# Where the split weights lie in the on-chip memory: stationary ones 16 bytes off a multiple of 256 from the activations

## The chip, the cores and the metric

The kernel runs on one core of a Trainium2 chip. A core has a matrix engine (TensorE, PE in the profile, with its weight loads as PEld), a vector engine (DVE), a scalar engine (ACT), GpSimd (POOL), a queue engine that issues transfers (SP), and an on-chip memory of 128 partitions in which every tile is given a byte address that is the same in all partitions. The metric is the device time of one execution in microseconds (us). What a measurement of this kernel can tell from no change is about 0.2%, 3 us.

## What is computed

One layer of a transformer-like backbone on 256 latent tokens and 256 context tokens of width 2048, all in 32-bit floats:

```
mod   = silu(c) @ w_mod + b_mod              # six vectors; mod_c likewise from c_ctx
h     = rmsnorm(x) * (1 + ca) + sa ;  h_c likewise from ctx
p     = h @ w_in       # q, k, v, pooling input, gate logits; of h_c only k and v
mix   = (sigmoid(g_a) * (diff_attention(q, k, v) @ w_a_up)
       + sigmoid(g_b) * (multiscale_pool(p_pool) @ w_b_up)) @ w_o
x     = x + ga * mix
x     = x + gm * (relu(h2 @ w_ff1)^2 @ w_ff2),   h2 = rmsnorm(x) * (1 + cm) + sm
```

w_ff1 is 2048 x 8192 and w_ff2 8192 x 2048. Together the weights are some 340 MB, read once.

## The kernel before

**Split products.** The matrix engine works here on a reduced form of 32-bit numbers (F32R). To keep the accuracy, every weight chunk and every activation is split into a high half (ACT copies it into F32R, line 213 for weights) and a low half (DVE subtracts the high half from the source, line 214). A product is three matmuls: high by high, high by low, low by high, summed in a PSUM bank.

**Stream of weights.** A list, `stream`, holds all chunks of weights in the order of use, 128 partitions x 1024 numbers (4 KB in each partition) but for the small `pool_w`. `wchunk` hands out the next one and calls `load_next` so that two further chunks are loaded: a transfer into one of five `raw` tiles, the split into a tile `whi` and a tile `wlo`, each with three buffers used in turn (lines 211 and 212). Before a chunk's halves are written, the matmuls on the chunk three places earlier must be done. The chunks of the first key group go to a tile `first` instead.

**Two forms of matmul.** In a matmul one operand of 128 x 128 is loaded into the array first (stationary; the profile's LDWEIGHTS) and the other is streamed past it (moving). While one matmul streams, the load for the next goes on.

- *Weights moving.* `xstat` (lines 391 to 414), `mod_chunk` and `xmm` load activations as stationary operand and stream 512 columns of a weight half. This is so for w_m, w_q, w_k, w_v, the gates, w_a, w_b, w_o and w_ff2.
- *Weights stationary.* The pooling input (`pooling`, w_p, through `mm3`, lines 241 to 243), the first block of the MLP's first product (`ff1_first`, w_ff1a, also `mm3`) and its blocks 1 to 7 (`ff1`, w_ff1, lines 939 and 942) load 128 x 128 of a weight half and stream activations. In `ff1` one chunk gives eight matmuls of its high half with 512 columns (both halves of the activations, 256 tokens each, line 939) and then eight of its low half with 256 columns (line 942). A matmul of `mm3` streams 256 columns. `pool_w` is stationary too (`pool_out`), against the tiles `dh` and `dl`.

The order of the blocks of the MLP is first product of block b+1, then second product of block b (`ff2`, through `xstat`). In the middle of the kernel attention is interleaved with the projections.

**Addresses.** A pool gives each tag of tiles (all its buffers) one piece of the partition, in the order in which the tags first occur, each buffer rounded up to 32 bytes. In order: the parameters, two tiles of 8 KB (`s8`), seven of 16 KB (`s16`: all split activations, hL, hC, h2, mix, oT, yb and act, lie in them), then `ones` (512 bytes), `ebias` and `epsb` (4 bytes each), `mean` (512), nine `work` tiles of 2048 (`dh`, `dl`, `ah`, `al` among them), `sil` (128), twelve small tiles of 64 bytes, `tabs` (2048), `wkt` (256), `nlam` and `sub8` (4 each), two `aT` tiles of 4096, five `raw` tiles of 4096, three `whi` and three `wlo` of 4096, and `macc`. From the end of the seven large tiles to the first `whi` these are 51,456 bytes, 201 x 256. So all halves of weights lie at a multiple of 256 bytes from all split activations. The work tiles lie 512 + 32 + 32 + 512 = 1088 bytes behind the large ones, 64 more than a multiple of 256.

Of the kernel before, what the change touches and what calls it, by code (L numbers as in the profile page):

```python
# [11 lines left out]
F32 = mybir.dt.float32  # L12
F32R = mybir.dt.float32r
# [4 lines left out]
P = 128  # L18
D = 2048
KT = D // P  # L20
# [28 lines left out]
def layer(ctx: ExitStack, tc, a, out):  # L49
    nc = tc.nc  # L50
    pool = ctx.enter_context(tc.tile_pool(name="sb", bufs=1))
# [23 lines left out]
    def s16(name, shape, dt=F32):  # L75
        return pool.tile(shape, dt, tag="s16", name=name, bufs=7)

    def s8(name, shape, dt=F32):
        return pool.tile(shape, dt, tag="s8", name=name, bufs=2)

    def small(name, n):
        return pool.tile([P, n], F32, tag="sm", name=name, bufs=12)

    def pairtile(name):
        return s16(name, [P, 2, 8, T], F32R)
# [25 lines left out]
    def raw_chunk(src, n=1024):  # L111
        raw = pool.tile([P, n], F32, tag="raw", name="raw", bufs=5)
        nc.sync.dma_start(raw, src)
        return raw
# [66 lines left out]
    def x1_tile():  # L181
        if not x1s:
            x1s.append(s16("x1", [P, 2, D]))
        return x1s[0]

    loaded = []
    done = [0]

    def load_next():
        key, rate = stream[len(loaded)]  # L190
        src = a[key[0]]
        for i in key[1:]:
            src = src[i]
        if key[0] == "prq":
            nc.sync.dma_start(prq, src)
            loaded.append((key, None, None))
            return
        if key[0] in ("cT", "x"):
            dst = cT[:, 4 * key[1]:4 * key[1] + 4, :] if key[0] == "cT" else x1_tile()[:, key[1], key[2] * 512:key[2] * 512 + 512]
            nc.sync.dma_start(dst, src)  # L200
            loaded.append((key, None, None))
            return
        n = src.shape[-1]
        raw = raw_chunk(src, n)
        if key[:2] == ("w_k", 0):
            if not first:
                first.append(s16("first", [P, 4, 1024], F32R))
            i = 2 * (key[2] % 2)
            hi, lo = first[0][:, i, :], first[0][:, i + 1, :]
        else:  # L210
            hi = pool.tile([P, n], F32R, tag="whi", name="whi", bufs=3)
            lo = pool.tile([P, n], F32R, tag="wlo", name="wlo", bufs=3)
        act.copy(hi, raw)  # L213
        vec.tensor_sub(lo, raw, hi.bitcast(F32))  # L214
        loaded.append((key, hi, lo))
        credit[0] += rate
        credit_rate[0] = rate
        while credit[0] >= 1.0:
            credit[0] -= 1.0
            if late[0] is not None:  # L220
                next(late[0], None)

    def wchunk(*key, ahead=AHEAD):
        while len(loaded) < min(done[0] + 1 + ahead, len(stream)) or loaded[done[0]][1] is None:
            if loaded and done[0] < len(loaded) and loaded[done[0]][1] is None:
                done[0] += 1
                continue
            load_next()
        got, hi, lo = loaded[done[0]]
        assert got == key, (got, key)  # L230
        loaded[done[0]] = None
        done[0] += 1
        tick()
        return hi, lo
# [10 lines left out]
    def rsq(v, n, div, tag=None):  # L245

        mk = (lambda nm: small(nm, n)) if n <= 16 else (lambda nm: work(nm, [P, n]))
        y = pool.tile([P, n], F32, tag=tag, name=tag, bufs=2) if tag else mk("rq_y")
        pin(act.activation(y, v, AF.Ln, scale=div * 2.0 ** -64, bias=epsb))
        act.activation(y, y, AF.Exp, scale=-0.5, bias=ebias)  # L250
        t = mk("rq_t")
        vec.scalar_tensor_tensor(t, y, -0.5 * div, y, ALU.mult, ALU.mult)
        vec.scalar_tensor_tensor(t, v, EPS / div, t, ALU.add, ALU.mult)
        vec.scalar_tensor_tensor(y, t, 1.5, y, ALU.add, ALU.mult)
        return y
# [4 lines left out]
    nc.sync.dma_start(prm, a["prm"])  # L260
    xT = s16("xT", [P, KT, T])
    cT = s16("cT", [P, KT, T])
    for i in range(4):
        nc.sync.dma_start(xT[:, 4 * i:4 * i + 4, :], a["xT"][i])

    def pr(name):
        lo, hi = PRM[name]
        return prm[:, lo:hi]
# [5 lines left out]
    ident = pr("ident")  # L274
    ones = pool.tile([P, P], F32R, tag="ones", name="ones")
    vec.memset(ones.bitcast(F32), 1.0)
    ebias = pool.tile([P, 1], F32, tag="ebias", name="ebias")
    vec.memset(ebias, -32.0 * math.log(2.0))
    epsb = pool.tile([P, 1], F32, tag="epsb", name="epsb")
    vec.memset(epsb, EPS * 2.0 ** -64)  # L280
    mean = pool.tile([P, P], F32, tag="mean", name="mean")
    vec.memset(mean, 1.0 / P)
# [2 lines left out]
    sg = work("sg", [P, 32])  # L285
    act.activation(sg, prm[:, PRM["c"][0]:PRM["cc"][1]], AF.Sigmoid)
    tc.keep_in_program_order(act.preload_act_table_set("natural_log_exp_and_others"))
    sil = pool.tile([P, 2, KT], F32, tag="sil", name="sil")
    vec.tensor_mul(sil.rearrange("p a k -> p (a k)"), sg, prm[:, PRM["c"][0]:PRM["cc"][1]])
    cv = s8("cv", [P, KT, P], F32R)  # L290
    vec.memset(cv.bitcast(F32), 0.0)
# [1 line left out]
    act.copy(cv[:, :, 0:2], silk)  # L293
    vec.tensor_sub(cv[:, :, 2:4], silk, cv[:, :, 0:2].bitcast(F32))
    b1 = small("b1", 16)
    vec.tensor_scalar(b1, pr("bca"), 1.0, None, ALU.add)

    tabs = pool.tile([P, 4, 2, 64], F32, tag="tabs", name="tabs")
    wkt = pool.tile([P, 64], F32, tag="wkt", name="wkt")
    nlam = pool.tile([P, 1], F32, tag="nlam", name="nlam")  # L300

    sub8 = pool.tile([P, 1], F32, tag="sub8", name="sub8")
    vec.tensor_scalar(sub8, pr("subln"), 1.0 - LAM0, None, ALU.mult)

    def tables():

        vec.tensor_copy(wkt, pq("wk"))

        vec.tensor_scalar(pq("wq"), pq("wq"), 0.125, None, ALU.mult)
        for i, w in enumerate(("wq", "wk")):  # L310
            wv = pq(w)
            for t in range(2):
                vec.tensor_mul(tabs[:, 2 * i, t, :], pq("cos")[:, t * 64:t * 64 + 64], wv)
                so = tabs[:, 2 * i + 1, t, :].rearrange("p (a b f) -> p a b f", a=2, b=2)
                si = pq("sin")[:, t * 64:t * 64 + 64].rearrange("p (a b f) -> p a b f", a=2, b=2)
                wr = wv.rearrange("p (a b f) -> p a b f", a=2, b=2)
                for b in range(2):
                    vec.tensor_mul(so[:, :, b, :], si[:, :, b, :], wr[:, :, 1 - b, :])
        lm = work("lm", [P, 2, 64])
        lam2 = small("lam2", 2)  # L320
        for i in range(2):
            vec.tensor_mul(lm[:, i, :], pq(f"lq{i + 1}"), pq(f"lk{i + 1}"))
        vec.reduce_sum(lam2, lm, axis=AX.X)
        act.activation(lam2, lam2, AF.Exp)
        vec.tensor_sub(nlam, lam2[:, 1:2], lam2[:, 0:1])
        vec.tensor_scalar(nlam, nlam, -LAM0, None, ALU.add)
# [765 lines left out]
```

## Time and profile before

| | |
|---|---|
| three runs | 1519.75, 1520.18, 1520.29 us, median 1520.18 |
| profiled execution | 1519.78 us |
| its span, first to last instruction | 1517.7 us, mean granted clock 0.994 |
| PE busy | 1480.7 us of matmuls, 98% of the span |
| DVE, ACT, POOL busy | 1063.2, 755.7, 129.3 us |
| moved by DMA | 347.82 MB, mean 229 GB/s |

Matmuls are pipelined and the profile models their ends, so the durations of matmul records overlap. What tells the pace of the matrix engine is the distance from one start to the next, read from the timeline (columns: start, duration, engine, line, operation, tiles, shapes, count of merged instructions). A row of a group gives count, busy time, mean duration in ns and idle time before. A row of the windows gives the stretch, its length, the busy time of each engine with its count, the granted clock, the share of the DMA engines and GB/s.

### The profile page before, as it was taken

What the parts mean: (1) busy time and instruction counts of PE and PEld (TensorE: products, weight loads), DVE (VectorE), ACT (ScalarE), POOL (GpSimd) and SP (SyncE); (2) the same over time, 40 slices, a digit from 0 to 9 for tenths busy, and PEclk for the clock granted to TensorE, in tenths of its full rate; (3) what the DMA queues carried; (4) which work ended last, traced back from release to release, by engine and by line L of the source; (5) the groups of instructions that cost most, each with busy time, mean ns of one, the idle gap of its engine ahead of it and who ended that gap; (6) DMA issues with size and microseconds to landing.
All of it is one profiled execution on the core that took longest, in us unless ns stands there. A gap on an engine that the chain in (4) does not pass through costs nothing.

```text
span 1517.7 us, 19767 instructions
## 1 busy us (share of the span) xinstructions
PE 1480.7 (98%) x7336; PEld 1232.8 (81%) x7336; DVE 1063.2 (70%) x1280; ACT 755.7 (50%) x1007; POOL 129.3 (9%) x124
## 2 busy tenths in 40 slices
PE   7899999999989999999999999999999999999998
PEld 5677877768878888888879988888888888888887
DVE  7799878777887767666757665666666555555675
ACT  6677534556655444444444554544444454444432
POOL 0100111000140000000000100100000000000170
PEclk9899999999999999999999999999999999999999
DMA  8888668556568787788755677767777666666664
GB/s 314 310 283 308 214 215 285 177 167 193 167 216 300 254 275 272 242 295 296 235 181 168 220 251 245 232 217 244 231 241 240 202 188 193 193 187 193 184 200 142
DMA packets 97439, 347.82 MB, mean 229 GB/s; under 512 B 11072, under 2 KB 11712, under 8 KB 97344
## 3 DMA queue, kind: packets, MB, share of 16 engines
q1 hardware_dynamic: 96768, 345.49, 70.4%
q8 instruction: 57, 0.93, 0.3%
q0 software_dynamic: 576, 1.08, 0.2%
q14 instruction: 38, 0.31, 0.1%
HBM read 344.44 MB, written 2.10 MB: 228 GB/s over the span
## 4 chain that ended last, share of the span: by engine, by line
PE 88%; issue 3%; DVE 3%; DMA 3%; ACT 1%; POOL 1%; DVEq 0%; SPq 0%; ACTq 0%; POOLq 0%
PE f L939 14%; PE f L411 8%; PE f L410 8%; PE f L413 8%; PE f L942 7%; PE pg L413 4%; PE pg L410 4%; PE pg L411 4%; PE pyy L410 2%; PE wo L410 2%; PE wo L413 2%; PE wo L411 2%; PE pyy L413 2%; PE pyy L411 2%; PE v L411 2%
## 5 line engine op out<-in xcount | busy, mean ns | idle before, releaser
L214 DVE TENSOR_TENSOR wlo<-raw,whi 128x1024 fp32r<-128x1024 f32 x507 | 628.6, 1244 | 365.2 <-ACT whi L213 350.9
L213 ACT CAST whi<-raw 128x1024 fp32r<-128x1024 f32 x507 | 529.8, 1047 | 587.3 <-PE f L411 178.1
L939 PE MATMUL f<-h,whi 128*128 128x512 f32 x896 | 224.2, 392 | 0.0
L411 PE MATMUL f<-whi,act 128*128 128x512 f32 x512 | 199.3, 389 | 0.0
L410 PE MATMUL f<-whi,act 128*128 128x512 f32 x512 | 199.3, 389 | 0.0
L939 PEld LDWEIGHTS f<-h,whi 128*128 128x128 f32 x896 | 161.5, 189 | 29.1
L588 DVE SCALAR_TENSOR_TENSOR macc<-raw,sil,macc 128x1024 f32<-128x1024 f32 x128 | 166.2, 1299 | 1.4 <-DMA raw<-in_w_cm_dram 0.8
L413 PE MATMUL f<-wlo,act 128*128 128x512 f32 x512 | 136.8, 389 | 0.0
L942 PEld LDWEIGHTS f<-h,wlo 128*128 128x128 f32 x896 | 122.2, 190 | 8.7
L942 PE MATMUL f<-h,wlo 128*128 128x256 f32 x896 | 124.9, 282 | 0.0
L413 PEld LDWEIGHTS f<-wlo,act 128*128 128x128 f32 x512 | 96.1, 188 | 20.0
L411 PEld LDWEIGHTS f<-whi,act 128*128 128x128 f32 x512 | 96.1, 188 | 19.8
L410 PEld LDWEIGHTS f<-whi,act 128*128 128x128 f32 x512 | 96.1, 188 | 19.8
L410 PE MATMUL pg<-whi,hL 128*128 128x512 f32 x256 | 100.5, 393 | 0.0
L411 PE MATMUL pg<-whi,hL 128*128 128x512 f32 x256 | 99.7, 389 | 0.0
L950 POOL TENSOR_TENSOR rsq<-relu 128x512 f32<-128x512 f32 x28 | 29.2, 1042 | 537.6 <-ACT relu L949 516.7
L413 PE MATMUL pg<-wlo,hL 128*128 128x512 f32 x256 | 68.6, 390 | 2.5 <-DVE wlo L214 2.5
L413 PEld LDWEIGHTS pg<-wlo,hL 128*128 128x128 f32 x256 | 48.0, 188 | 12.9 <-DVE wlo L214 2.9
L410 PEld LDWEIGHTS pg<-whi,hL 128*128 128x128 f32 x256 | 48.1, 188 | 10.1 <-issue 0.2
L411 PEld LDWEIGHTS pg<-whi,hL 128*128 128x128 f32 x256 | 48.1, 188 | 10.1 <-issue 0.2
L410 PE MATMUL wo<-whi,mix 128*128 128x512 f32 x128 | 49.9, 390 | 0.0
L411 PE MATMUL wo<-whi,mix 128*128 128x512 f32 x128 | 49.8, 389 | 0.0
(267 smaller groups left out, 2205.1 us busy)
## 6 DMA issues: line engine op xcount, KB each, us to landing
raw<-in_w_ff_dram SPq DMA_DIRECT2D x240, 512.0 KB, 4.3
raw<-in_w_m_dram SPq DMA_DIRECT2D x64, 512.0 KB, 4.9
raw<-in_w_ga_dram SPq DMA_DIRECT2D x32, 512.0 KB, 4.6
raw<-in_w_cm_dram SPq DMA_DIRECT2D x32, 512.0 KB, 4.6
raw<-in_w_gb_in_dram SPq DMA_DIRECT2D x32, 512.0 KB, 4.5
raw<-in_w_ga_in_dram SPq DMA_DIRECT2D x32, 512.0 KB, 4.4
raw<-in_w_sm_dram SPq DMA_DIRECT2D x32, 512.0 KB, 4.7
raw<-in_w_o_dram SPq DMA_DIRECT2D x32, 512.0 KB, 4.6
```

Source lines behind the costliest of these rows:

```text
L213: act.copy(hi, raw)
L214: vec.tensor_sub(lo, raw, hi.bitcast(F32))
L410: pe.matmul(banks[t], tok(h, k, 0, tt), wt, start=k == 0, stop=False)
L411: pe.matmul(banks[t], tok(h, k, 1, tt), wt, start=False, stop=False)
L413: pe.matmul(banks[t], tok(h, k, 0, tt), wt, start=False, stop=k == 2 * nk - 1)
L588: pin(vec.scalar_tensor_tensor(acc, raw, sil[:, 0, k:k + 1], acc, ALU.mult, ALU.add))
L939: pe.matmul(ps, hi[:, kk * P:kk * P + P], both(h2, k), start=k == 0, stop=False)
L942: pe.matmul(ps[:, T:2 * T], lo[:, kk * P:kk * P + P], act_slice(h2, k, 0), start=False, stop=k == KT - 1)
L950: gp.tensor_mul(sq, r, r)
```

## The change

The order of the instructions in the source and the operations are the same; the places of tiles change.

- `whi` and `wlo` become six tags of one buffer each, 1028 numbers (4112 bytes) wide. The chunks still take them in turn, three of each. A chunk's halves start at number 0 of their tile, or at number 4 (16 bytes) if the weights are w_p, w_ff1a or w_ff1.
- The six tags are allocated right behind the seven large tiles. Between them lie small ones: four tags of three small tiles (before one tag of twelve; `small` now takes the four in turn), `ebias`, `epsb`, `nlam`, `sub8`, and `sil` widened to 224 bytes. A half tile takes 4128 bytes rounded up, three small tiles 192 and a column 32: 4352 = 17 x 256. With `sil` it is 4128 + 224 = 4352 too.
- Allocations named `place` only fix that order; nothing is written to them.

So w_p, w_ff1a and w_ff1 lie 16 bytes beyond a multiple of 256 from the activations, and all other weights in these tiles at a multiple of 256, as before. What comes behind the six tags moves: the work tiles, `aT`, `raw` and `macc` are then 32 bytes off a multiple of 256 from the large tiles.

```diff
@@ -78,8 +78,11 @@
+    smalls = [0]
+
     def small(name, n):
-        return pool.tile([P, n], F32, tag="sm", name=name, bufs=12)
+        smalls[0] += 1
+        return pool.tile([P, n], F32, tag=f"sm{smalls[0] % 4}", name=name, bufs=3)
@@ -186,6 +189,16 @@
+    STATIONARY, OFFSET = ("w_p", "w_ff1a", "w_ff1"), 4
+    chunks = [0]
+
+    def halves(n, at):
+
+        i = chunks[0] % 3
+        chunks[0] += 1
+        return [pool.tile([P, 1028], F32R, tag=f"{part}{i}", name=part, bufs=1)[:, at:at + n] for part in ("whi", "wlo")]
+
@@ -208,8 +221,7 @@
-            hi = pool.tile([P, n], F32R, tag="whi", name="whi", bufs=3)
-            lo = pool.tile([P, n], F32R, tag="wlo", name="wlo", bufs=3)
+            hi, lo = halves(n, OFFSET if key[0] in STATIONARY else 0)
@@ -260,6 +272,15 @@
+    columns = []
+    for i, name in enumerate(("ebias", "epsb", "nlam", "sub8", "sil")):
+        pool.tile([P, 1028], F32R, tag=f"{('whi', 'wlo')[i // 3]}{i % 3}", name="place", bufs=1)
+        if i < 4:
+            pool.tile([P, 16], F32, tag=f"sm{i}", name="place", bufs=3)
+        columns.append(pool.tile([P, 1 if i < 4 else 56], F32, tag=name, name=name))
+    ebias, epsb, nlam, sub8, sil = columns
+    sil = sil[:, 0:32].rearrange("p (a k) -> p a k", a=2)
@@ -274,9 +295,7 @@
-    ebias = pool.tile([P, 1], F32, tag="ebias", name="ebias")
-    epsb = pool.tile([P, 1], F32, tag="epsb", name="epsb")
@@ -285,7 +304,6 @@
-    sil = pool.tile([P, 2, KT], F32, tag="sil", name="sil")
@@ -297,9 +315,7 @@
-    nlam = pool.tile([P, 1], F32, tag="nlam", name="nlam")
-
-    sub8 = pool.tile([P, 1], F32, tag="sub8", name="sub8")
```

## The prediction

> **What bounds the kernel now.** I read the engine rows of the page first, then the costliest groups of matmuls.
>
> ```profile
> span 1517.7 us, 19767 instructions
> ...
> PE 1480.7 (98%) x7336; PEld 1232.8 (81%) x7336; DVE 1063.2 (70%) x1280; ACT 755.7 (50%) x1007; POOL 129.3 (9%) x124
> ...
> GB/s 314 310 283 308 214 215 285 177 167 193 167 216 300 254 275 272 242 295 296 235 181 168 220 251 245 232 217 244 231 241 240 202 188 193 193 187 193 184 200 142
> ...
> L939 PE MATMUL f<-h,whi 128*128 128x512 f32 x896 | 224.2, 392 | 0.0
> L411 PE MATMUL f<-whi,act 128*128 128x512 f32 x512 | 199.3, 389 | 0.0
> ...
> L942 PE MATMUL f<-h,wlo 128*128 128x256 f32 x896 | 124.9, 282 | 0.0
> ```
>
> ```profile
> L241 PE MATMUL pin<-hL,whi 128*128 128x256 f32 x128 | 37.5, 293 | 0.0
> L241 PE MATMUL f<-h,whi 128*128 128x256 f32 x128 | 37.3, 296 | 0.7 <-ACT h L65 0.7
> ```
>
> PE is busy for 98% and its matmuls in the stages of the change have no idle time ahead of them. So what counts is the distance between starts. The stages whose weights are stationary, as stretches (length, then PE, PEld, DVE, ACT and POOL busy, clock, DMA share, GB/s):
>
> ```profile
> 363.00:430.00 67.00, 63.15 (x455) 56.02 (x454) 58.61 (x81) 40.01 (x70) 18.09 (x30) 1.00 0.62 195
> ```
>
> ```profile
> 801.00:803.20 2.20, 2.20 (x12) 2.20 (x12) 2.20 (x3) 0.07 (x1) 0.00 (x0) 0.51 0.30 32
> 804.50:849.50 45.00, 45.00 (x380) 45.00 (x379) 28.30 (x31) 19.70 (x24) 0.52 (x1) 1.00 0.68 209
> 850.15:894.84 44.69, 44.69 (x258) 39.32 (x257) 31.95 (x34) 25.74 (x36) 7.21 (x7) 1.00 0.71 230
> ```
>
> In turn: the pooling input, the start and the body of the first MLP block, and one of the blocks 1 to 7 (16 chunks in 44.69 us, 2.793 us a chunk). In the last two PE is busy throughout, while DVE idles for 13 to 17 us, ACT for 19 to 25, and the DMA engines for about 30%. Now the timeline of two chunks of block 1, and the first chunk of block 2, which follows a stretch of the other form:
>
> ```profile
> 850.15 2.00 PE L939 MATMUL f<-h,whi 128*128 128x512 f32 x8
> 851.99 1.11 PE L942 MATMUL f<-h,wlo 128*128 128x256 f32 x8
> 852.95 2.00 PE L939 MATMUL f<-h,whi 128*128 128x512 f32 x8
> 854.79 1.12 PE L942 MATMUL f<-h,wlo 128*128 128x256 f32 x8
> 855.74 2.00 PE L939 MATMUL f<-h,whi 128*128 128x512 f32 x8
> ```
>
> ```profile
> 938.39 1.98 PE L939 MATMUL f<-h,whi 128*128 128x512 f32 x8
> 940.21 1.12 PE L942 MATMUL f<-h,wlo 128*128 128x256 f32 x8
> 941.16 2.00 PE L939 MATMUL f<-h,whi 128*128 128x512 f32 x8
> ```
>
> Eight matmuls of 512 columns take 1.84 us (230 ns each) behind matmuls of 256 columns, but 1.82 us (227 ns) behind a stretch of 512. Same instructions, same tiles, same full clock, idle nowhere: the pace depends on how the streams of the loads and of the moving operand stand to each other. Eight of 256 columns take 0.95 us, 119 ns each. With weights moving the pace is 1.81/8 = 0.2265 us for 512 columns:
>
> ```profile
> 985.81 0.39 PE L410 MATMUL f<-whi,act 128*128 128x512 f32 x1
> ...
> 987.62 1.07 PE L413 MATMUL f<-wlo,act 128*128 128x512 f32 x4
> ```
>
> The trace has the same form with other places of its tiles. In `pool_out` the moving `dh`, `dl` stand 64 bytes past a multiple of 256 from the stationary halves, by the order of allocation; the pooling input beside it stands at a plain multiple:
>
> ```profile
> 421.24 0.28 PE L241 MATMUL pd<-dh,whi 128*128 128x256 f32 x1
> ...
> 421.92 0.28 PE L241 MATMUL pin<-hL,whi 128*128 128x256 f32 x1
> ...
> 423.42 0.28 PE L243 MATMUL pin<-hL,wlo 128*128 128x256 f32 x1
> ...
> 424.98 0.60 PE L665 MATMUL aTp<-prm,e 128*128 128x128 f32 x4
> ```
>
> Six matmuls at 64 bytes in 421.92 - 421.24 = 0.68 us are 113 ns each; thirteen at 0 in 424.98 - 423.42 = 1.56 us are 120 ns each. The same 64 bytes with 512 columns (`ah`, `al` against `ones` and, for the load behind, hL) go the other way, 0.24 us each against 0.226:
>
> ```profile
> 244.37 0.40 PE L599 MATMUL late<-ah,ones 128*128 128x512 f32 x1
> 244.61 0.40 PE L600 MATMUL late<-al,ones 128*128 128x512 f32 x1
> 244.85 0.39 PE L410 MATMUL k<-whi,hL 128*128 128x512 f32 x1
> ```
>
> So the distance of the tiles may matter by 6% either way. At half clock nothing is lost: the first MLP block starts at a granted 0.51, and seven matmuls take 1.49 us, 213 ns each, which at full clock would be half, 107 ns.
>
> ```profile
> 801.32 0.41 PE L242 MATMUL f<-h,whi 128*128 128x256 f32 x1
> ...
> 802.81 0.41 PE L241 MATMUL f<-h,whi 128*128 128x256 f32 x1
> ```
>
> **The change part by part.** *Nothing removed or added.* The same 507 splits, transfers and 7336 matmuls run in the same order on each queue; no wait is added, and each half tile is still free again after three chunks, each small one after twelve. These edits cost 0. If a wait did come of it, the chunk behind would be late, and the cover is the idle time of ACT ahead of its splits, which ends when PE frees a half:
>
> ```profile
> ACT whi L213 <- PE f L939: 84.2, 66, 1.7
> ```
>
> 84.2 us over 66 waits are 1.3 us a wait, so up to about that much is hidden.
>
> *Moved tiles behind the halves.* `raw` now stands 32 bytes off the halves, so a split reads and writes at other distances. The trace has DVE subtractions at a distance of 0 (`wlo<-raw,whi`, 1024 columns) and of 64 (`al<-macc,ah`, 512 columns):
>
> ```profile
> L214 DVE TENSOR_TENSOR wlo<-raw,whi 128x1024 fp32r<-128x1024 f32 x503 | 625.5, 1248 | 365.2 <-ACT whi L213 350.9 <-ACT v L616 3.7 <-PE k L413 2.5
> ...
> L238 DVE TENSOR_TENSOR al<-macc,ah 128x512 fp32r<-128x512 f32 x16 | 10.6, 685 | 0.0
> ```
>
> 1.22 ns a column at 0 against 1.34 at 64 with its start-up shared by half the columns: no sign that DVE minds the distance. I take 0. If all of that were the distance, a split would cost 10% of 1248 ns, 0.12 us a chunk more or, for the other sign, less; in the MLP the 13 us that DVE idles in 16 chunks hide it, and without that cover 0.12 x 507 = 61 us would be at stake.
>
> *Weights moving.* Their distance stays 0: 0.
>
> *Weights stationary, 16 bytes off.* No row shows 16 bytes. For 256 columns the bounds are 107 ns (half-clock row at full clock) and 129 (120 as now, and 9 ns, by which the 512-column pair at 64 bytes is slower). For 512 columns they are 213 (twice 107) and 236 (that pair: 0.24 by its rounded starts; 0.235 by the modelled durations, 397 against 389 ns):
>
> ```profile
> L599 PE MATMUL late<-ah,ones x16: 397/397/501, 244.4 to 1188.1; 128*128 128x512 f32 x16
> ```
>
> (The columns are the shortest, median and longest of 16, in ns.) I take 113 and 227: these are the paces that occur in this trace wherever the streams stand well, at 64 bytes for the one and behind 512-column stretches for the other, and they are one rate, 113.3 ns for 256 columns. At 120 the load looks like the limit: 119 to 120 comes only where one load must be done per 256 columns, so a load that is held up less should bring 113.
>
> Sum at the likeliest, against the profiled 1519.78 us:
> - Blocks 1 to 7: 896/8 = 112 chunks. A chunk would take 8 x 0.2267 + 8 x 0.1133 = 2.720 us in place of 2.793, 0.073 less: 112 x 0.073 = 8.2 us.
> - First block: 3 x 8 x 16 = 384 matmuls, some 24 of them at low clock; 360 x 0.0067 = 2.4 us.
> - Pooling input: again 384, 2.6 us if all of it shows. The chain of waits there:
>
> ```profile
> by line: PE pin L243 12.0%; PE pin L242 11.8%; PE pin L241 11.8%; issue 8.5%; PE ob L674 7.7%; PE sc L646 6.3%; DMA raw<-in_w_p_dram 5.3%; DVE wlo L214 4.8%; DVE macc L588 4.3%; PE aTp L665 4.2%; POOL zb L744 1.9%; DVE mx L647 1.8%; POOL za
> ```
>
> 35.6% of 67 us, 24 us, of the 384 x 0.12 = 46 us lie on it, about half: 1.3 us. The rest is covered by DVE (58.61 of 67 us busy) and the weights of w_p.
> - Together 11.9 us: 1519.78 - 11.9 = 1507.9. The profiled run lies 0.4 us under the median of the three, so I say 1508. What is late next in the MLP is nothing: at 2.720 us a chunk the transfers need 230 x 2.793/2.720 = 236 GB/s, and the slices of the page's GB/s row reach 314.
>
> **The rivals.**
> 1. *The distance does not matter.* The loss of 7 ns per 256 columns (120 against 113) belongs to the rhythm of load and stream, not to addresses, and pool_out's 113 ns came from its start. For it: pool_out never has more than a dozen matmuls in a row, and the steady 120 may need more. Against it: the equal instructions above at 227 and 230, and the pair at 236. The same time follows if the allocation doesn't land where the sums of sizes say. Nothing then changes in the sum: 1519.8 us. The Trainium skill, page "TensorE: Matmul & The Clock Gate", section "Step-by-step: what each phase is for", says that PE has two independent read ports into the on-chip memory and that loading the next weights takes no read bandwidth from the running matmul; by that rule it would be this rival, and the trace's 227 and 230 ns of the same instruction do not agree with it.
> 2. *The offset meets the moving stream* (other side). The load's reads then fall where the moving stream reads, as in the moved pair. Place: line 939. At 236 ns and with line 942 left at 120, a chunk takes 1.888 + 0.960 = 2.848 us, 0.055 more, 112 x 0.055 = 6.2 us: 1526. If the 256-column ones rise by 9 ns too, 0.127 us in a chunk, 14.2 us, and 0.009 x (360 + 192) = 5.0 us in the others: 1539. It decides from where line 939 loses more than line 942 gains. For it the 0.24 us; against it, that these are two lone matmuls each time, with no rhythm found yet.
> 3. *All loss goes.* At 107 and 213 ns a chunk takes 2.560 us: 112 x 0.233 = 26.1, first block 360 x 0.0133 = 4.8, pooling half of 5.1: 33 us, 1486. For it only the half-clock row; against it, that neither 0 nor 64 bytes shows less than 113.
>
> **How the numbers follow.** Chances: forecast (1502 to 1514) 0.50; no change (within 3 us) 0.17; slower 0.22; all loss gone or most of it 0.11. Faster by over 0.2% (3 us, about what a measurement of this kernel can tell from no change): 0.50 + 0.11 = 0.61; within: 0.17; slower: 0.22. The range leaves out the 0.11 at 1486 and the tail of rival 2 beyond 1527 (0.05): 1500 to 1527. The likeliest case alone: 1502 to 1514. Predicted: 1508.
>
> **What would show it.** Right: the eight of line 942 span 0.91 us in the timeline in place of 0.95, those of line 939 1.81 in place of 1.84; a block's 16 chunks span 43.5 us in place of 44.69; the pooling input 113 ns apart; lines 410 to 413 at 0.2265 as before. Wrong: line 942 at 0.95 and 939 at 1.84 (rival 1), line 939 at 1.88 or more (rival 2), 1.71 and 0.86 (rival 3), or a block faster with ACT or DVE as the new wait ahead of line 939. DVE's split far from 1248 ns would break the second part.

## The result, and the profile after

| | before | after |
|---|---|---|
| median of the runs | 1519.97 us (4 runs, 1518.35 to 1520.29) | 1528.76 us (4 runs, 1524.93 to 1529.34) |
| profiled execution | 1519.78 us | 1524.93 us |
| mean of span x mean granted clock | 1508.0 us (23 executions, those beside the first experiments) | 1508.6 us (4 executions) |

After over before is 1.0056, with a 95% interval of 1.0043 to 1.0068: slower by 8.8 us, outside the predicted range and of the other sign. The profiled execution of after is the fastest of its four, so its trace accounts for 5.1 of the 8.8 us. The last row of the table is explained below: at one and the same clock the two kernels would take nearly the same time.

The page of after, its engine rows and the costliest groups that answer to those shown of before (the lines of the source have moved: the splits are 225 and 226, `mm3` 253 to 255, `ff1` 955 and 958):

```profile
PE 1483.3 (97%) x7336; PEld 1233.9 (81%) x7336; DVE 1062.7 (70%) x1280; ACT 754.9 (50%) x1007; POOL 128.2 (8%) x124
...
L226 DVE TENSOR_TENSOR wlo<-raw,whi 128x1024 fp32r<-128x1024 f32 x507 | 628.9, 1244 | 369.4 <-ACT whi L225 354.3
...
L955 PE MATMUL f<-h,whi 128*128 128x512 f32 x896 | 222.1, 390 | 0.0
...
L958 PE MATMUL f<-h,wlo 128*128 128x256 f32 x896 | 124.2, 281 | 0.0
```

The same number of matmuls and splits, and the groups of the change a little shorter: line 955 2.1 us, line 958 0.7. But PE fell from 98% to 97% of a longer span (1522.8 us). Something outside these groups became slower.

**The MLP gained, a third of what was predicted.** The timeline of after, chunks of block 1 and of block 2:

```profile
857.99 2.03 PE L955 MATMUL f<-h,whi 128*128 128x512 f32 x8
859.86 1.11 PE L958 MATMUL f<-h,wlo 128*128 128x256 f32 x8
860.81 2.02 PE L955 MATMUL f<-h,whi 128*128 128x512 f32 x8
...
946.50 1.98 PE L955 MATMUL f<-h,whi 128*128 128x512 f32 x8
948.31 1.11 PE L958 MATMUL f<-h,wlo 128*128 128x256 f32 x8
949.26 1.98 PE L955 MATMUL f<-h,whi 128*128 128x512 f32 x8
```

In blocks 2 to 7 the eight of line 955 now take 1.81 us from start to start, as predicted, and a chunk 2.76. But the eight of line 958 still take 0.95 us, not 0.91. And block 1, with the same addresses and the same instructions, found another rhythm: 1.87 + 0.95 = 2.82, slower than before's 2.793. Over the blocks 1 to 7, by the starts of line 942 (958 after) in the views of tile f:

```profile
L942 PE MATMUL f<-h,wlo x896: 277/283/283, 852.0 to 1425.9; 128*128 128x256 f32 x180
```

```profile
L958 PE MATMUL f<-h,wlo x896: 277/281/283, 859.9 to 1431.0; 128*128 128x256 f32 x180
```

573.9 us became 571.1: a gain of 2.8 us. And these rows show that block 1 began 7.9 us late.

**The loss is in the first stage.** There the matmuls of w_k, w_q and w_m (the modulation, `mod`) are interleaved. The rows of tile w_q, before and then after, with the first and the last start:

```profile
L243 PE MATMUL w_q<-whi,hL x32: 387/389/397, 36.5 to 168.0; 128*128 128x512 f32 x32
```

```profile
L255 PE MATMUL w_q<-whi,hL x32: 388/389/397, 35.9 to 176.3; 128*128 128x512 f32 x32
```

The last product of w_q is 8.3 us later. The windows of before and of after over this stage, 66 to 170 us (columns as in the prediction; the two short stretches of after are used below):

```profile
66.00:170.00 104.00, 101.45 (x446) 79.10 (x445) 94.25 (x166) 73.72 (x102) 0.00 (x0) 1.00 0.83 288
```

```profile
66.00:170.00 104.00, 95.38 (x399) 70.63 (x398) 88.29 (x150) 68.42 (x93) 0.00 (x0) 0.98 0.82 276
...
133.50:138.20 4.70, 2.35 (x8) 0.98 (x7) 3.61 (x6) 2.12 (x3) 0.00 (x0) 1.00 0.94 363
138.20:142.20 4.00, 3.97 (x10) 3.15 (x11) 3.58 (x6) 3.25 (x6) 0.00 (x0) 0.57 0.57 216
```

PE does 399 matmuls in the same 104 us in which it did 446, and is idle for 8.6 us instead of 2.6. What it waits for stands in the waits of this stretch, before and then after (who waits, for whom; us in total, times, longest):

```profile
ACT whi L213 <- PE w_q L243: 2.1, 2, 1.1
ACT whi L213 <- PE mod L347: 1.8, 4, 0.7
...
PEld mod L347 <- ACT whi L213: 1.1, 2, 0.6
```

```profile
PEld mod L363 <- ACT whi L225: 7.8, 10, 1.6
...
ACT whi L225 <- PE mod L363: 7.1, 6, 2.7
...
ACT whi L225 <- PE w_q L255: 4.9, 3, 3.9
```

ACT, which splits the chunks, now waits 12.0 us for matmuls to give back a half tile (3.9 us before), and the loads of PE wait 7.8 us for ACT (1.1 before). The chunk behind does come late, at a place where PE has nothing else ready.

**Behind some of the waits the clock falls.** The timeline of PE in after around the short stretches above (idle time before an instruction and its releaser in brackets):

```profile
135.56 0.73 PE L363 MATMUL mod<-whi,cv 128*128 128x512 f32 x2 [1.18 <-ACT whi L225]
136.82 0.73 PE L363 MATMUL mod<-wlo,cv 128*128 128x512 f32 x2 [0.53 <-DVE wlo L226]
138.23 0.92 PE L363 MATMUL mod<-whi,cv 128*128 128x512 f32 x2 [0.67 <-ACT whi L225]
138.94 0.63 PE L253 MATMUL w_k<-first,hL 128*128 128x512 f32 x1
139.37 0.63 PE L254 MATMUL w_k<-first,hL 128*128 128x512 f32 x1
```

Three waits of 0.5 to 1.2 us leave PE busy for 2.35 of 4.70 us; then the granted clock is 0.57 for 4 us, and matmuls start 0.43 us apart in place of 0.23. The profiled execution of before has the clock at 1.00 in all of 66 to 170 us. The Trainium skill, page "TensorE: Matmul & The Clock Gate", section "Why this matters for your kernels", asks to avoid idle gaps of PE of more than about 3 us between bursts; here no single gap is above 1.2 us and the clock fell.

Not every wait has this effect. In the pooling stage PE waits for ACT about as long in before as in after (timeline, before and then after), but the clock falls behind the wait in after alone (windows, in the same order):

```profile
404.62 0.66 PE L665 MATMUL aTp<-prm,e 128*128 128x128 f32 x4 [2.44 <-ACT e L651]
```

```profile
410.42 0.66 PE L681 MATMUL aTp<-prm,e 128*128 128x128 f32 x4 [2.55 <-ACT e L667]
```

```profile
405.80:409.20 3.40, 3.40 (x28) 3.26 (x28) 2.62 (x5) 1.99 (x4) 3.17 (x9) 1.00 0.33 113
```

```profile
411.70:415.10 3.40, 3.40 (x18) 3.40 (x17) 1.91 (x5) 1.19 (x3) 3.29 (x7) 0.50 0.38 130
```

This execution of after has three such stretches of half clock that before's lacks, at 138.6, 411.7 and 452.6 us, of some 3.4 us each. By estimate (half of 3.4 us) each costs 1.7 us; only the first of them lies in the first stage.

The clock is also what differs most between executions of one kernel. The span times the mean granted clock of the same execution is about what the span would be if all of it ran at full clock, since PE is busy for 97 to 98% of it. For six executions of a_off0 (below), which took from 1524.15 us (clock 0.994) to 1533.84 us (clock 0.987), this product is 1512.0 us with a standard deviation of 0.5: what differs between them is the clock. Of before the mean clock is 0.9936, of after 0.9888. So of the 8.0 us by which the mean span of after is longer (1525.8 against 1517.8), 0.6 us are in the product; the 0.0048 of clock times 1526 us is 7.3.

### The profile page after: what moved, and what is told of

Read it like the earlier page. It is cut to its first block, busy times and chain, and to the rows that moved or that the text cites. A ratio compares the mean times of both kernels' runs of the same rounds, so it can differ in the third digit from the quotient of the medians.

```text
span 1522.8 us, 19769 instructions
## 1 busy us (share of the span) xinstructions
PE 1483.3 (97%) x7336; PEld 1233.9 (81%) x7336; DVE 1062.7 (70%) x1280; ACT 754.9 (50%) x1007; POOL 128.2 (8%) x124
## 4 chain that ended last, share of the span: by engine, by line
PE 88%; DVE 4%; DMA 3%; ACT 2%; issue 2%; POOL 1%; DVEq 0%; SPq 0%; ACTq 0%; POOLq 0%
PE f L955 13%; PE f L427 8%; PE f L426 8%; PE f L429 8%; PE f L958 7%; PE pg L429 4%; PE pg L426 4%; PE pg L427 4%; DVE wlo L226 2%; PE v L426 2%; PE v L427 2%; PE v L429 2%; PE wo L429 2%; PE pyy L427 2%; PE pyy L429 2%; PE wo L426 2%
## 5 line engine op out<-in xcount | busy, mean ns | idle before, releaser
L226 DVE TENSOR_TENSOR wlo<-raw,whi 128x1024 fp32r<-128x1024 f32 x507 | 628.9, 1244 | 369.4 <-ACT whi L225 354.3
L427 PEld LDWEIGHTS pg<-whi,hL 128*128 128x128 f32 x256 | 48.2, 188 | 10.3 <-issue 0.5
L363 PE MATMUL mod<-whi,cv 128*128 128x512 f32 (+1 forms) x144 | 43.3, 391 | 7.7 <-ACT whi L225 7.5
L426 PE MATMUL wo<-whi,mix 128*128 128x512 f32 x128 | 49.9, 390 | 0.0
```

The costliest lines, as they stand in the source:

```text
L363: pe.matmul(ps[:, 0:n], cv[:, k, :], part[:, kk * n:kk * n + n], start=(k == 0 and part is hi), stop=(k == 15 and part is lo))
L426: pe.matmul(banks[t], tok(h, k, 0, tt), wt, start=k == 0, stop=False)
L427: pe.matmul(banks[t], tok(h, k, 1, tt), wt, start=False, stop=False)
```

## The experiments

The edits are shown by their main lines.

The question was first which of the two parts costs the time: the places of the tiles, or that the buffers have names. The kernel before has three buffers under one tag, and a chunk gets whichever of them is free; the kernel after has three tags of one buffer and takes them in a fixed turn. In the program of before the numbers of the `whi` buffers run 0210210210210210102102102020120120..., not always in turn. (That three buffers are used in turn, as the section on the kernel before has it, is so only after the change.) Where a chunk of w_q is held long, since its products are spread over several chunks of w_m, the other two buffers alternate past it.

**r_halves: the kernel before, with only the halves in named buffers taken in turn.** Addresses modulo 256 stay as they were.

```diff
-            hi = pool.tile([P, n], F32R, tag="whi", name="whi", bufs=3)
-            lo = pool.tile([P, n], F32R, tag="wlo", name="wlo", bufs=3)
+            i = chunks[0] % 3; chunks[0] += 1
+            hi, lo = [pool.tile([P, 1024], F32R, tag=f"{part}{i}", name=part, bufs=1)[:, 0:n] for part in ("whi", "wlo")]
```

> The kernel before, all tiles at their old addresses modulo 256, with one edit: high and low halves in three named buffers each, taken in turn, in place of any free one of three. Theory: the whole early loss of the changed kernel, 6 to 12 us over the first 170 us, time 1526 to 1532; MLP blocks as before at 44.67. Rival (buffers in turn cost nothing, the loss comes from addresses or from the small tiles): 1519 to 1522.

Measured: 1531.59 us (5 runs, 1525.69 to 1533.73), ratio 1.0078 (1.0065 to 1.0091). The windows of r_halves and its row of w_q:

```profile
66.00:170.00 104.00, 96.22 (x404) 71.48 (x403) 89.36 (x153) 69.33 (x95) 0.00 (x0) 0.98 0.83 278
...
74.00:78.00 4.00, 4.00 (x13) 3.17 (x13) 4.00 (x14) 2.55 (x5) 0.00 (x0) 0.57 0.82 282
```

```profile
L243 PE MATMUL w_q<-whi,hL x32: 387/389/402, 35.4 to 175.1; 128*128 128x512 f32 x32
```

The whole loss is there with no address moved modulo 256: 404 matmuls, PE idle for 7.8 us, the clock at 0.57 from 74 to 78 us, the last product of w_q at 175.1. Of the 10.6 us by which the mean span is longer, 3.9 are in the product of span and clock (1511.9 against 1508.0); the rest is clock (0.9892).

**r_small: the kernel before, with only the twelve small tiles as four groups of three.**

```diff
-        return pool.tile([P, n], F32, tag="sm", name=name, bufs=12)
+        count[0] += 1; return pool.tile([P, 16], F32, tag=f"sm{count[0] % 4}", name=name, bufs=3)[:, 0:n]
```

> The kernel before with one edit: the twelve small tiles as four groups of three taken in turn, in place of one group of twelve; no other tile moves. Theory: little or nothing, 1518 to 1522. Rival (the small tiles make the loss): 1526 to 1530.

Measured: 1520.04 us (11 runs), ratio 1.0001 (0.9992 to 1.001). Its window:

```profile
66.00:170.00 104.00, 100.62 (x443) 78.52 (x442) 93.43 (x164) 71.94 (x100) 1.33 (x1) 1.00 0.81 279
```

Nearly the work of before (443 matmuls), and the clock stays at 1.00. The small tiles cost nothing that can be measured. (This kernel, too, has stretches of half clock in the pooling and behind it: a mean clock of 0.91 in 394 to 414 and in 435 to 455 us.)

**a_off0: the kernel after, with the 16 bytes set to 0.** The instructions keep the order of after.

```diff
-    STATIONARY, OFFSET = ("w_p", "w_ff1a", "w_ff1"), 4
+    STATIONARY, OFFSET = ("w_p", "w_ff1a", "w_ff1"), 0
```

> The changed kernel with the one number OFFSET set from 4 to 0: same order of all instructions as the changed kernel, but the halves of the stationary weights at a plain multiple of 256 bytes from the activations. Theory (two separate effects: the 16 bytes quicken the matmuls of the MLP by about 3 us, and tying each chunk to one of three named buffers in turn makes the first 170 us some 8 to 12 us slower): the early loss stays, the pace of blocks 2 to 7 goes back from 44.16 to 44.67 us a block, time 1531 to 1533, ratio to the kernel before 1.007 to 1.009. Rival (the 16 bytes themselves cost the time, say by splits that start off a line): time back to 1519 to 1521.

Measured: 1532.83 us (6 runs, 1524.15 to 1533.84), ratio 1.0068 (1.0048 to 1.0089). Its timeline in block 3:

```profile
1045.75 2.00 PE L955 MATMUL f<-h,whi 128*128 128x512 f32 x8
1047.59 1.11 PE L958 MATMUL f<-h,wlo 128*128 128x256 f32 x8
1048.54 2.00 PE L955 MATMUL f<-h,whi 128*128 128x512 f32 x8
```

The chunk is back at 1.84 + 0.95 = 2.79 us, so the 16 bytes alone make the difference of pace. The intervals of the two ratios overlap, because of the clock; span times clock separates them: 1512.0 us against 1508.6 for after. The offset is worth 3.4 us. All that after lost, it lost without the offset.

**m_all: the tiles where after has them, 16 bytes included, but each chunk takes the buffer that it had before.** The numbers come from a written list (`whi` 0210210210210210102102..., `wlo` and the small tiles likewise).

```diff
-            hi = pool.tile([P, n], F32R, tag="whi", name="whi", bufs=3)
-            lo = pool.tile([P, n], F32R, tag="wlo", name="wlo", bufs=3)
+            at = {"whi": 4, "wlo": 4} if key[0] in ("w_p", "w_ff1a", "w_ff1") else {"whi": 0, "wlo": 0}
+            hi, lo = [pool.tile([P, 1028], F32R, tag=f"{part}{next(taken[part])}", name=part, bufs=1)[:, at[part]:at[part] + n] for part in ("whi", "wlo")]
```

> The changed kernel's addresses, 16 bytes included, but each chunk takes the buffer that the kernel before gave it (a written list of buffer numbers for high halves, low halves and small tiles in place of taking them in turn). Theory (the loss is the fixed turn of the buffers): the first 170 us run as before, the gain in the MLP stays, time 1515 to 1518, ratio 0.997 to 0.999; blocks 2 to 7 at 44.16 us. Rival (the moved tiles or the 16 bytes cost the time): 1525 to 1530 as in the changed kernel.

Measured: 1517.43 us (11 runs, 1513.28 to 1519.85), ratio 0.9981 (0.9971 to 0.9991). Its window of the first stage, its row of w_q, and two chunks of block 2 (this kernel and those below have the line numbers of before):

```profile
66.00:170.00 104.00, 101.31 (x445) 78.59 (x444) 94.00 (x165) 73.36 (x102) 0.00 (x0) 1.00 0.81 284
```

```profile
L243 PE MATMUL w_q<-whi,hL x32: 387/389/397, 35.4 to 167.9; 128*128 128x512 f32 x32
```

```profile
940.53 1.98 PE L939 MATMUL f<-h,whi 128*128 128x512 f32 x8
942.34 1.11 PE L942 MATMUL f<-h,wlo 128*128 128x256 f32 x8
943.29 1.98 PE L939 MATMUL f<-h,whi 128*128 128x512 f32 x8
```

With the choice of buffers restored, the first stage is that of before to within one matmul and 0.1 us, and the gain of the offset is left: span times clock is 1504.1, 3.9 us under before's. Its MLP has after's two rhythms, 44.96 us for block 1 and 44.16 for each of the others, against 44.69 and 44.67 before. So the two parts of the change are told apart: named buffers in a fixed turn cost some 11 us, the 16 bytes gain 3 to 4.

**Other distances.** The 16 bytes had not brought 113 ns, so the next question was which distance does, and whether each group of matmuls has its own pace at its own distance. All of these are m_all with other numbers in `at`, wider tiles where they are needed, and halves of the other weights still at a multiple of 256 from the activations. m_off8, m_off16 and m_offm16 put all stationary weights 32, 64 and -16 bytes off; m_off16b is m_off16 once more; m_hi has 16 bytes for the high halves and 0 for the low ones.

```diff
m_off8    at = {"whi": 8, "wlo": 8}
m_off16   at = {"whi": 16, "wlo": 16}
m_offm16  at = {"whi": 4, "wlo": 4}, all others {"whi": 8, "wlo": 8}
m_hi      at = {"whi": 4, "wlo": 0}
```

> The kernel m_all with 32 bytes in place of 16 for w_p, w_ff1a and w_ff1. What is asked is the pace alone, read from the timeline of the MLP blocks. Theory (the read streams of the load and of the moving operand settle into a rhythm that depends on their distance, and 113 ns per 256 columns is reached only at some distances): another rhythm than at 0 or 16 bytes, eight matmuls of line 942 anywhere from 0.907 to 0.965 us, eight of line 939 from 1.81 to 1.88. Rival (any distance but 0 breaks the standstill at 120 in the same way): as m_all, 1.813 + 0.947 us.

> m_all with 64 bytes in place of 16 (the small columns stand in other places, so that the six halves still lie at multiples of 256). This is the distance at which the kernel before ran six pooling matmuls 113 ns apart. Theory (113 belongs to this distance): line 942 at 0.907 us, line 939 at 1.81 or, as in the lone pair of 512 columns, 1.88. Rival (those six were too few to settle): line 942 at 0.94 to 0.96 us.

> m_all with the stationary halves 16 bytes short of a multiple of 256 in place of 16 beyond. Theory (distance decides, with sign): a rhythm of its own, line 942 between 0.907 and 0.965 us, line 939 between 1.81 and 1.88. Rival (what counts is only that the streams do not start in one line): as m_all, 1.813 + 0.947.

> m_all with the 16 bytes for the high halves only; the low halves stand at 0. Theory (each group keeps the rhythm of its own distance): line 942 back to 0.953 us, line 939 at 1.813 or with a start-up loss of up to 0.03. Rival (the gain of line 939 comes only from the phase in which line 942 leaves the streams): line 939 back to 1.841 too.

> The same kernel as m_off16, timed in rounds beside m_mix4. From its profile (first block 113.7 ns, blocks 2 to 7 at 44.42 us): 1515 to 1517, ratio 0.997.

Measured, with the pace of a steady chunk in blocks 2 to 7 (eight of line 939 + eight of line 942) and the pace of the matmuls of 256 columns in the first block (from the fifth matmul on of a stretch without others between):

| distance | kernel | us | chunk, us | block, us | first block, ns each |
|---|---|---|---|---|---|
| 0 | before | 1519.97 | 1.841 + 0.952 = 2.793 | 44.67 | 119.9 |
| 16 | m_all | 1517.43 | 1.813 + 0.947 = 2.760 | 44.16 | 118.4 |
| 32 | m_off8 | 1526.12 (one run) | 1.861 + 0.952 = 2.813 | 45.01 | 118.3 |
| 64 | m_off16 | 1515.32 (one run) | 1.862 + 0.912 = 2.774 | 44.42 | 113.3 |
| 64 | m_off16b | 1516.78, ratio 0.9976 (0.9967 to 0.9985) | 1.862 + 0.912 = 2.774 | 44.42 | 113.3 |
| -16 | m_offm16 | 1517.0 (one run) | 1.843 + 0.937 = 2.780 | 44.45 | 117.4, in one stretch 119.9 |
| 16 high, 0 low | m_hi | 1522.12 (one run) | 1.857 + 0.956 = 2.813 | 44.97 | 117.9 |

The run of m_off8 had a clock of 0.989, so only 2.4 us of its excess (7 x 0.34) are the pace of its blocks. 16 bytes beyond a multiple of 256 and 16 short of one give different paces, so the sign counts. (m_hi, with the buffers of before, also loses the clock once in the first stage: 0.57 from 124 to 128 us, behind a wait of 1.50 us.) The timeline of m_off16, block 3:

```profile
1029.90 2.02 PE L939 MATMUL f<-h,whi 128*128 128x512 f32 x8
1031.76 1.07 PE L942 MATMUL f<-h,wlo 128*128 128x256 f32 x8
1032.67 2.02 PE L939 MATMUL f<-h,whi 128*128 128x512 f32 x8
```

At 64 bytes the matmuls of 256 columns run at 114 ns and those of 512 columns at 233 (1.86 us for eight, where 1.81 or 1.88 was expected), just as the two odd pairs of rows in the trace of before had it (`pool_out` and `late`). At 16 bytes it is the other way round, 227 and 118. m_hi spoils the plain picture. Its timeline, block 2:

```profile
950.20 2.02 PE L939 MATMUL f<-h,whi 128*128 128x512 f32 x8
952.06 1.12 PE L942 MATMUL f<-h,wlo 128*128 128x256 f32 x8
953.01 2.02 PE L939 MATMUL f<-h,whi 128*128 128x512 f32 x8
```

The high halves lie at 16 bytes, where all-16 gave 1.81 us, and take 1.86; the low ones lie at 0 and take 0.956 in place of 0.952. A group does not keep the pace of its own distance when the group beside it lies at another.

**m_mix4 and m_mix0: the best pace of each group.** Low halves of w_ff1 and both of w_p and w_ff1a at 64 bytes; high halves of w_ff1 at 16 bytes in the one and 0 in the other. The edit of m_mix4 against m_off16:

```diff
-            at = {"whi": 16, "wlo": 16} if key[0] in ("w_p", "w_ff1a", "w_ff1") else {"whi": 0, "wlo": 0}
+            at = {"whi": 16, "wlo": 16} if key[0] in ("w_p", "w_ff1a") else {"whi": 4, "wlo": 16} if key[0] == "w_ff1" else {"whi": 0, "wlo": 0}
```

> The kernel m_off16 with one more distinction: w_p and w_ff1a and the low halves of w_ff1 at 64 bytes, the high halves of w_ff1 at 16. From the runs so far: 64 bytes give 114 ns per 256 columns (line 942 0.912 us for eight), 16 bytes 1.813 us for eight of line 939. Theory (each group runs at the pace of its own distance): 1.813 + 0.912 = 2.725 us a chunk, 7.6 us off the MLP, first block 2.2 us off, time 1509 to 1512. Rival (as m_hi suggests, the two groups disturb each other's rhythm): line 939 at 1.84 to 1.87, time 1514 to 1517.

> As m_mix4, but the high halves of w_ff1 at 0 bytes. Theory of own pace: 1.813 to 1.841 + 0.912 us a chunk. Rival (mutual disturbance): line 939 above 1.841 or line 942 above 0.92.

Measured: m_mix4 1519.45 us (11 runs, ratio 0.9994, 0.9985 to 1.0003), m_mix0 1519.21 (one run). The timeline of m_mix4, block 3:

```profile
1033.16 2.03 PE L939 MATMUL f<-h,whi 128*128 128x512 f32 x8
1035.02 1.11 PE L942 MATMUL f<-h,wlo 128*128 128x256 f32 x8
1035.96 2.03 PE L939 MATMUL f<-h,whi 128*128 128x512 f32 x8
```

If each group kept its own pace, a chunk of m_mix4 would take 1.813 + 0.912 = 2.725 us. It takes 1.864 + 0.942 = 2.806, more than at either distance alone; m_mix0 takes 1.838 + 0.942. The theory of an own pace falls.

**m_best: one distance for each stage.** 64 bytes where all matmuls have 256 columns (w_p and w_ff1a), 16 bytes for both halves of w_ff1. Its line of distances:

```diff
+            at = {"whi": 16, "wlo": 16} if key[0] in ("w_p", "w_ff1a") else {"whi": 4, "wlo": 4} if key[0] == "w_ff1" else {"whi": 0, "wlo": 0}
```

> The kernel m_off16 with w_p and w_ff1a left at 64 bytes (114 ns per 256 columns) and both halves of w_ff1 at 16 (1.813 + 0.947 us a chunk in blocks 2 to 7 of m_all). Theory (a stage whose matmuls are all of one distance keeps the pace found for it): first MLP block 2.2 us faster than before, blocks 2 to 7 at 44.16 us, block 1 anywhere from 44.16 to 44.96 by the phase in which it starts, the pooling up to 1 us faster; together 5 to 6.5 us, time 1513.5 to 1515.5, ratio 0.996 to 0.997. Rival (what one stage gains is lost in the others, as in m_off16 whose gates were 2 us later): 1516 to 1518.

Measured: 1514.98 us (8 runs, 1511.92 to 1518.26) against 1519.5 of before in the same comparison (12 runs), ratio 0.9969 (0.9957 to 0.9981). It is faster than before and than after. Of its first block, the row of line 241 in the view of tile f, of before and of m_best:

```profile
L241 PE MATMUL f<-h,whi x128: 277/283/580, 799.2 to 849.8; 128*128 128x256 f32 x128
```

```profile
L241 PE MATMUL f<-h,whi x128: 275/277/581, 799.2 to 847.4; 128*128 128x256 f32 x128
...
L942 PE MATMUL f<-h,wlo x896: 277/282/284, 849.6 to 1420.8; 128*128 128x256 f32 x180
```

The first block is 2.4 us shorter (50.6 to 48.2; 360 matmuls at 6.6 ns less would be 2.4), blocks 1 to 7 2.7 us (573.9 to 571.2). Span times clock is 1501.7 us, 6.2 under before's 1507.9; its mean clock was 0.9926 against 0.9936, which gave 1.5 us back.

## Why the prediction was wrong, step by step

- **"These edits cost 0"** is the step that failed. The instructions did not run in the same order on each queue, and a half tile was not still free after three chunks: with names, the chunk three places behind a held one must wait for just that buffer, where before it took another. The queues came out in another order, too: by line and tiles, 362 of PE's 7336 places hold another matmul than before, the first at 66 us (318 in r_halves, all between 66 and 208 us). Cost: 11.7 us by the medians of r_halves and its before. The bound that the prediction gave for a wait, 1.3 us of cover, came from the waits of the MLP, where each chunk is used up in turn. The stage in which chunks are held was not looked at, and there PE has 2.6 us of idle time in 104, so a late chunk goes straight into the end. Part of this was in the text of the source: `bufs=3` against three names is a change in who may have which buffer, not a rename.
- **The clock was not in the sum.** Stage one was at a granted 1.00 before; in the profiled executions of after and r_halves it has 0.98, in that of a_off0 0.95 (some 2 and 5 of 104 us). Over all executions the lower clock makes 6.7 of r_halves's 10.6 us of mean span; the waits at full clock make 3.9. Since stretches of half clock stand in other stages and in other kernels too, it isn't shown that all of the 6.7 us come from the waits of the first stage.
- **16 bytes off, 113 and 227 ns.** Right in sign, wrong in size. Line 939 ran at 227 as said, in six of seven blocks. Line 942 ran at 118 and not at 113: the 113 was read at 64 bytes and used for 16. Blocks 1 to 7 gave 2.8 us in place of 8.2 (6 x 0.51 less the 0.27 that block 1 lost), the first block about 0.5 in place of 2.4 (50.0 us from its first matmul to the first of line 955, against 50.5 in a_off0; before has 51.0, but also a longer start at half clock). The pooling input gained nothing that can be seen: 72.2 us from its first to its last matmul of line 253, 72.3 in a_off0. Together 3.4 to 3.9 us in span times clock, in place of 11.9. At one clock this nearly cancels the 3.9 us of waits, which is why the product of after is only 0.6 us above that of before. Without the fixed turn (m_all) the time did fall, but by 2.5 us and not by 12. The two rows of 64 bytes were read rightly: m_off16 has both of their paces, 114 and 233.
- **Weights moving: 0, and DVE: 0.** Right: line 427 has 389 ns a matmul against 389 of line 411, and line 226 has 1244 ns a split against 1248. But a premise was wrong, in what the section on the change says of places. The loop places five of the six tags of halves, the sixth lies behind `raw`, and by the sums of sizes `raw` and `aT` stay at a plain multiple of 256 from the large tiles. So a split's distance changed only by the 16 bytes of the stationary weights (1221 ns a split in block 1, 1223 before); 32 bytes were not tested. And the work tiles came to a plain multiple, from 64 bytes past one, since `ebias` and `epsb` no longer lie ahead of them. The trace of after agrees: nine matmuls of `pool_out` in a row now take 1.06 us, 118 ns each, in place of the 113 that the prediction read, and the `late` matmuls show a median of 389 ns in place of 397.

```profile
427.20 0.28 PE L253 MATMUL pd<-dh,whi 128*128 128x256 f32 x1
...
428.26 0.28 PE L253 MATMUL pin<-hL,whi 128*128 128x256 f32 x1
```

Here the moving tiles were displaced and the halves of `pool_w` were not. That speaks for the distance between the two as the cause, and not the address of the weights alone; at the other distances only the weights were moved.

- **Rival 1, the distance does not matter:** falls. Five distances give five paces of a chunk, from 2.760 to 2.813 us, for the same instructions at full clock.
- **Rival 2, slower since the load meets the moving stream:** the right side, by another mechanism. A distance that costs does exist (32 bytes, 2.813 us), but after was not slower for that.
- **Rival 3:** no run shows a pace under 113 ns at full clock.

What stays open: by which rule a distance gives its rhythm, and why block 1 falls into another one than blocks 2 to 7. Whether the first stage lost by the waits themselves or by the new order of the queues wasn't tried apart. Nor is it shown why one execution loses the clock in a place where another keeps it. One thing in the traces may bear on it: within an execution the stretches of half clock begin whole multiples of some 3.41 us apart (43.0, 138.6, 411.7, 452.6 and 804.2 us in after). If the clock is set once in such an interval, a wait would count by how much of it falls into one interval; no run tested that.

## What to carry to other kernels

Giving the buffers of one tag names and a fixed turn takes away a freedom; before costing it at nothing, look for the stage in which a chunk is held longer than its turn, and read the cover there, not in the steadiest stage. A price read at one distance is a price for that distance: what 64 bytes do says nothing of 16. And compare span times granted clock beside the span: it tells in a few executions what the clock's scatter of some 10 us hides.

## What was not expected of the hardware

- The pace of F32R matmuls with back-to-back loads depends on the byte distance between the stationary and the moving tiles (counted here modulo 256; no other modulus was tested): 113.3 to 119.9 ns for 256 columns and 227 to 233 for 512, with the clock at 1.00 and no idle time.
- It is a rhythm of the whole sequence. At 16 bytes block 1 settles at 2.81 us a chunk and the next six at 2.76; and two distances in turn (m_mix4, 2.806) can be slower than each of them alone (2.760 and 2.774).
- Short waits, none above 1.2 us, that leave PE half idle over some 4.7 us were followed by 4 us at a granted 0.57; a wait of 2.44 us in before was not, and one of 2.55 us in after was (0.50 over 3.4 us).
